# A two-block transformer forward pass: the feed-forward transposes go from TensorE to VectorE and device memory

## The chip, the cores and the metric

The kernel runs on one core of a Trainium2 chip. The metric is the device time of one execution in microseconds. A core has a matrix engine (TensorE, in the rows PE, with PEld for its weight loads), two engines for elementwise work that the kernel uses all the time (VectorE: DVE; ScalarE: ACT), a third one (GpSimd: POOL), an engine that here only issues transfers (SyncE: SP), and 16 DMA engines that move data between device memory and the on-chip memory (SBUF). TensorE writes into PSUM, eight banks of 128 x 512 floats.

## The reference

Two blocks run one after the other on 256 tokens of width 1024, all in float32. The first has a recurrent mixer and a differential attention, a feed-forward network with a squared ReLU (1024 to 4096 to 1024) and a gated embedding. The second has two layers, and each is a gated feed-forward network, an attention mixer and a second gated feed-forward network. The part that the change touches is this one, four times the gated form and once the squared ReLU:

```python
D_FF_2 = 2816
def swiglu(x, w_gate, w_up, w_down):
    return (jax.nn.silu(x @ w_gate) * (x @ w_up)) @ w_down

x = x + jnp.square(jax.nn.relu(h @ w_ff1[i])) @ w_ff2[i]            # first block, once
x = x + 0.5 * swiglu(rms_norm(x, norm_ffn1[layer]), w_gate, w_up, w_down)   # second block, four times
```

## The kernel before

**Products in three parts.** Each float32 product is made of three matrix products on a reduced type: an operand is split into `hi` (ScalarE copies it with rounding, L373) and `lo` (VectorE subtracts, L374), and TensorE adds hi x hi, lo x hi and hi x lo (`mm3`, all at L287).

**Weights.** They stream from device memory in units of 128 x 1024 floats (512 KB). SyncE issues the load into one of three `raw` buffers (L349), ScalarE and VectorE split it into `hi` and `lo`, and 11 pairs of those buffers stand ready for TensorE. A raw buffer comes free when `lo` is made, a pair when TensorE has used it for the last time.

**The feed-forward network (`mlp`).** The hidden width is cut into chunks: eight of 512 for the squared ReLU, and 512, 512, 512, 256, 512, 512 for each gated one. For each chunk TensorE makes a pass of 24 matrix products for each of the two token tiles t = 0, 1 and each of the input matrices (gate and up, or the one of the squared ReLU). ScalarE applies the activation to the first result (`a`, L471), and VectorE multiplies it with the second (`a`, L473). The chunk's `a` has to be turned around before it can stand as the stationary operand of the down product: `flip_side` queues four 128 x 128 transposes on TensorE (`tr`, L291), which a later `mm3` lets in between two of its products; then ScalarE and VectorE split the result from PSUM into `aTh` and `aTl`. The down product of a chunk comes one chunk later (`held`), after that chunk's own passes; the last two chunks are done together at the end.

**What sets the order.** TensorE runs in the order in which the program emits its work. A small model of time in the program (`Weave`, with a clock `t` that each matrix product moves on) decides where a queued side piece such as a transpose is let in. The other engines' queues are ordered by the framework's scheduler, when the program is built.

Of the kernel before, what the change touches and what calls it, by code (L numbers as in the profile page):

```python
# [7 lines left out]
F32 = mybir.dt.float32  # L8
# [4 lines left out]
AF = mybir.ActivationFunctionType  # L13
ALU = mybir.AluOpType
# [94 lines left out]
class Mark:  # L109


    def __init__(self):
        self.done, self.at, self.res = False, 0.0, None
# [105 lines left out]
class Ker:  # L219


    def __init__(self, ctx, tc, d):
        self.tc, self.nc, self.d = tc, tc.nc, d
        nc = self.nc
        ctx.enter_context(tc.manual_schedule(engines={mybir.EngineType.PE}))
        self.W = Weave()
        self.const = ctx.enter_context(tc.tile_pool(name="const", bufs=1))
        self.small = ctx.enter_context(tc.tile_pool(name="small", bufs=2))
        self.line_up(ctx, "a", 48)
        self.xp = ctx.enter_context(tc.tile_pool(name="xp", bufs=1))  # L230
        self.act = ctx.enter_context(tc.tile_pool(name="act", bufs=2))
        self.ps = ctx.enter_context(tc.tile_pool(name="ps", bufs=1, space=PSUM))
        self.banks = Slots(self.W, self.ps, "b", [128, 512], 8)
        self.quota, self.held = 2, 0
        self.x = [self.xp.tile([128, D], F32, name=f"x{t}") for t in range(2)]
        self.pre = None
# [135 lines left out]
    def split(self, hi, lo, src):  # L372
        self.nc.scalar.activation(out=hi, in_=src, func=AF.Copy)  # L373
        self.nc.vector.tensor_tensor(out=lo, in0=src, in1=hi.bitcast(F32), op=ALU.subtract)  # L374
# [63 lines left out]
    def flip_side(self, src, hi, lo, lat, wait=()):  # L438
# [8 lines left out]
        s.res = (hi, lo)  # L447
        return s

    def mlp(self, pool, hT, names, i, chunks, kind, res, after):

        nc, W = self.nc, self.W
        self.quota = 6
        acc = {}
        held = []
        nw = len(names) - 1
        for ci, w in enumerate(chunks):
            kt = w // 128  # L460
            ws = [self.wblock((n, i, ci)) for n in names[:-1]]
            order = [(t, j) for t in range(2) for j in range(nw)] if ci == 0 else [(t, j) for j in range(nw) for t in range(2)]
            a, aT = {}, {}
            for t, j in order:
                b = self.bank()
                p = b[1][:, :w]
                for k in range(8):
                    self.mm3(p, hT[t].at(k), ws[j][k], k == 0, k == 7)
                if j == 0:
                    a[t] = pool.tile([128, 512], F32, tag="a", name="a", bufs=4)[:, :w]  # L470
                    nc.scalar.activation(out=a[t], in_=p, func=AF.Silu if kind == "swiglu" else AF.Relu, scale=hT[t].r)  # L471
                if j == nw - 1:
                    nc.vector.scalar_tensor_tensor(out=a[t], in0=p, scalar=hT[t].r, in1=a[t], op0=ALU.mult, op1=ALU.mult)  # L473
                    th = pool.tile([128, 4, 128], F32R, tag="aTh", name="aTh", bufs=5)
                    tl = pool.tile([128, 4, 128], F32R, tag="aTl", name="aTl", bufs=5)
                    aT[t] = self.flip_side(a[t], th[:, :kt], tl[:, :kt], 3.0)
                self.drop(b, 2.0)
            held.append((kt, aT, self.wblock((names[-1], i, ci))))
            if 1 <= ci < len(chunks) - 1:
                for t in range(2):  # L480
                    self.down(acc, t, held[:1], res)
                held = held[1:]
        for t in range(2):
            self.down(acc, t, held, res, after)
# [1378 lines left out]
```

## Time and profile before

| | us |
|---|---|
| three timed runs, median (lowest, highest) | 1516.84 (1516.67, 1520.73) |
| the profiled execution | 1517.79 |
| its span, first to last instruction | 1516.0 |
| TensorE busy, matrix products | 1473.4 (97%) |
| VectorE busy | 927.7 (61%) |
| ScalarE busy | 760.7 (50%) |
| GpSimd busy | 46.9 (3%) |

An engine's busy share says how much of the span it worked. Matrix products overlap at their ends, so TensorE's time is better read from when one product starts to when the next one does. The five feed-forward networks take 940.6 us of the span.

### The profile page before, as it was taken

To read this page: it belongs to the slowest core of one execution; us is meant where nothing else is said; L and a number is where in the kernel's file an instruction comes from. 1 tells how busy PE (TensorE), PEld (TensorE's weight loads), DVE (VectorE), ACT (ScalarE), POOL (GpSimd) and SP (SyncE) were. 2 spreads that over 40 slices of the span, in tenths; PEclk is the share of its full clock that TensorE was granted. 3 is DMA by queue.
4 is the path that set the end of the run, shared out by engine and by line. 5 is a ranking of instruction groups with operands and counts; after the bars stand their busy time and mean duration, and the time that the engine had idled before them with its cause. 6 is when DMAs were issued, how large, how long until landed. Compare 5 with 4: busy or idle time off the path is not lost.

```text
span 1516.0 us, 22441 instructions
## 1 busy us (share of the span) xinstructions
PE 1473.4 (97%) x8804; PEld 1235.3 (81%) x8804; DVE 927.7 (61%) x1529; ACT 760.7 (50%) x1142; POOL 46.9 (3%) x70
## 2 busy tenths in 40 slices
PE   7899988999999999999999999999999999999999
PEld 6887767888888778887888888887888878888887
DVE  5885778755558755558546554565545787565552
ACT  6644445544446544436665444445444566464441
POOL 1120100000000000001100000000000010000000
PEclk9999999999999999999999999999999999999999
DMA  7233338655554765545434756547565444276551
GB/s 254 87 121 108 101 113 272 203 191 187 181 167 140 229 204 193 186 145 195 137 101 140 220 184 196 187 146 235 183 195 189 139 158 128 82 223 193 177 186 55
DMA packets 76298, 254.97 MB, mean 168 GB/s; under 512 B 11040, under 2 KB 13344, under 8 KB 76192
## 3 DMA queue, kind: packets, MB, share of 16 engines
q1 hardware_dynamic: 76192, 253.53, 51.8%
q8 instruction: 69, 1.13, 0.3%
q14 instruction: 37, 0.30, 0.1%
HBM read 252.45 MB, written 1.05 MB: 167 GB/s over the span
## 4 chain that ended last, share of the span: by engine, by line
PE 79%; DVE 7%; DMA 6%; ACT 5%; issue 2%; SPq 0%; POOL 0%; ACTq 0%; DVEq 0%; POOLq 0%
PE b L287 75%; DMA raw<-in_w_dram 5%; PE b L291 4%; DVE lo L374 3%; ACT hi L373 2%; DMA grow<-in_norm_mix_g_dram 0%; DMA stage<-in_consts_dram 0%; DMA lam<-in_lam_k_dram 0%; ACT L380 0%; DVE c L1141 0%; POOL rb L572 0%; DVE U L1269 0%; POOL rb L571 0%; DVE u L1138 0%; ACT e L384 0%
## 5 line engine op out<-in xcount | busy, mean ns | idle before, releaser
L374 DVE TENSOR_TENSOR lo<-raw,hi 128x1024 fp32r<-128x1024 f32 (+1 forms) x465 | 562.0, 1215 | 356.1 <-ACT hi L373 347.1
L373 ACT ACTIVATE hi<-raw 128x1024 fp32r<-128x1024 f32 (+1 forms) x465 | 486.0, 1050 | 415.8 <-PE b L287 207.1
L287 PE MATMUL b<-hi,hTh 128*128 128x512 f32 (+2 forms) x1312 | 495.6, 378 | 0.5 <-ACT hi L373 0.5
L287 PE MATMUL b<-lo,hTh 128*128 128x512 f32 (+2 forms) x1312 | 484.7, 369 | 0.8 <-DVE lo L374 0.8
L287 PE MATMUL b<-hi,hTl 128*128 128x512 f32 (+2 forms) x1312 | 484.9, 370 | 0.1
L287 PEld LDWEIGHTS b<-hi,hTl 128*128 128x128 f32 x1312 | 247.5, 189 | 43.1 <-DVE hTl L374 0.6
L287 PEld LDWEIGHTS b<-hi,hTh 128*128 128x128 f32 x1312 | 247.6, 189 | 42.0 <-issue 2.7
L287 PEld LDWEIGHTS b<-lo,hTh 128*128 128x128 f32 x1312 | 248.0, 189 | 40.0 <-DVE lo L374 1.7
L287 PE MATMUL b<-hi,aTh 128*128 128x512 f32 x480 | 191.4, 399 | 0.0
L287 PE MATMUL b<-lo,aTh 128*128 128x512 f32 x480 | 187.3, 390 | 0.0
L287 PE MATMUL b<-hi,aTl 128*128 128x512 f32 x480 | 187.2, 390 | 0.0
L287 PEld LDWEIGHTS b<-hi,aTl 128*128 128x128 f32 x480 | 90.2, 188 | 19.8
L287 PEld LDWEIGHTS b<-lo,aTh 128*128 128x128 f32 x480 | 90.3, 188 | 17.4
L287 PEld LDWEIGHTS b<-hi,aTh 128*128 128x128 f32 x480 | 90.2, 188 | 17.5
L471 ACT ACTIVATE a<-b,rsi_x 128x512 f32<-128x512 f32 (+1 forms) x52 | 34.4, 662 | 54.0 <-PE b L287 54.0
L373 ACT ACTIVATE aTh<-b 128x512 fp32r<-128x512 f32 (+1 forms) x64 | 36.3, 567 | 39.5 <-PE b L291 38.5
L473 DVE SCALAR_TENSOR_TENSOR a<-b,rsi_x,a 128x512 f32<-128x512 f32 (+1 forms) x52 | 37.3, 717 | 28.4 <-PE b L287 15.9
L287 PE MATMUL b<-hi,hT1h 128*128 128x512 f32 (+1 forms) x128 | 53.5, 418 | 0.0
L374 DVE TENSOR_TENSOR aTl<-b,aTh 128x512 fp32r<-128x512 f32 (+1 forms) x64 | 41.8, 653 | 17.2 <-ACT aTh L373 16.9
L287 PE MATMUL b<-lo,hT1h 128*128 128x512 f32 (+1 forms) x128 | 47.7, 372 | 0.6 <-DVE lo L374 0.6
L287 PE MATMUL b<-hi,hT1l 128*128 128x512 f32 (+1 forms) x128 | 47.4, 371 | 0.0
L374 DVE TENSOR_TENSOR hTl<-b,hTh 128x512 fp32r<-128x512 f32 (+1 forms) x48 | 29.2, 619 | 23.5 <-ACT hTh L373 23.5
(583 smaller groups left out, 1289.0 us busy)
## 6 DMA issues: line engine op xcount, KB each, us to landing
raw<-in_w_dram SPq DMA_DIRECT2D x446, 512.0 KB, 4.2
raw<-in_w_dram SPq DMA_DIRECT2D x16, 384.0 KB, 3.4
grow<-in_norm_ffn_dram SPq DMA_DIRECT2D x4, 512.0 KB, 5.0
x<-in_x_dram SPq DMA_DIRECT2D x4, 256.0 KB, 5.5
x<-in_x_dram SPq DMA_DIRECT2D x2, 512.0 KB, 4.3
grow<-in_norm_mix_dram SPq DMA_DIRECT2D x2, 512.0 KB, 4.5
out_dram<-x SPq DMA_DIRECT2D x4, 256.0 KB, 2.0
raw<-in_w_dram SPq DMA_DIRECT2D x2, 396.0 KB, 3.5
```

The costliest lines, as they stand in the source:

```text
L287: self.nc.tensor.matmul(out=out, lhsT=lhsT, rhs=rhs, start=start, stop=stop, skip_group_check=skip)
L291: self.nc.tensor.transpose(out=out, in_=src, identity=self.ident)
L373: self.nc.scalar.activation(out=hi, in_=src, func=AF.Copy)
L374: self.nc.vector.tensor_tensor(out=lo, in0=src, in1=hi.bitcast(F32), op=ALU.subtract)
L471: nc.scalar.activation(out=a[t], in_=p, func=AF.Silu if kind == "swiglu" else AF.Relu, scale=hT[t].r)
L473: nc.vector.scalar_tensor_tensor(out=a[t], in0=p, scalar=hT[t].r, in1=a[t], op0=ALU.mult, op1=ALU.mult)
```

## The change

The `a` of most chunks no longer passes TensorE. `flip_moved` lets VectorE transpose the 32 x 32 blocks of `a` into a buffer `fsq`, GpSimd's queue writes that to a scratch tensor `fmid` in device memory, and four more transfers of GpSimd's queue, one for each 32 partitions, read it back into `fto` with the blocks in their transposed places. ScalarE and VectorE then split `fto` (in SBUF) instead of a PSUM bank. Those splits are emitted later, in the next chunk: before its second pass, or before its fourth in chunk 1 of a gated network. The last chunk of each network, and chunk 0 of the squared ReLU, keep TensorE's transposes. So 52 of 64 turned tiles change path: 44 of width 512 (four transposes each) and 8 of width 256 (two each), 192 transposes in all.

```diff
+        self.dram = ctx.enter_context(tc.tile_pool(name="dram", bufs=3, space=bass.MemoryType.DRAM))
+    def flip_moved(self, pool, src, hi, lo):
+        nc = self.nc
+        n = src.shape[1] // 128
+        sq = pool.tile([128, 4, 4, 32], F32, name="fsq", tag="fsq", bufs=2)[:, :, :n]
+        to = pool.tile([128, 4, 4, 32], F32, name="fto", tag="fto", bufs=2)[:, :, :n]
+        nc.vector.transpose(out=sq.rearrange("p j k s -> p k j s"), in_=src.rearrange("p (k j s) -> p k j s", j=4, s=32))
+        mid = self.dram.tile([4, 32, 4, 128 * n // 4], F32, name="fmid", tag=f"fmid{n}")
+        nc.gpsimd.dma_start(out=mid.rearrange("i r j e -> (i r) j e"), in_=sq.rearrange("p j k s -> p j (k s)"))
+        for j in range(4):
+            nc.gpsimd.dma_start(out=to[32 * j:32 * j + 32].rearrange("r i k s -> r i (k s)"), in_=mid[:, :, j].rearrange("i r e -> r i e"))
+        v = lambda x: x.rearrange("p k (i s) -> p i k s", s=32)
+        m = Mark()
+        def split():
+            nc.scalar.activation(out=v(hi), in_=to, func=AF.Copy)
+            nc.vector.tensor_tensor(out=v(lo), in0=to, in1=v(hi).bitcast(F32), op=ALU.subtract)
+            m.res = (hi, lo)
+            self.W.finish(m, 4.0)
+        m.split = split
+        return m
...
-            for t, j in order:
+            landed, moved = moved, []
+            for n, (t, j) in enumerate(order):
+                if n == (1 if ci > 1 else 3):
+                    for m in landed:
+                        m.split()
...
-                    aT[t] = self.flip_side(a[t], th[:, :kt], tl[:, :kt], 3.0)
+                    if ci == len(chunks) - 1 or ci < 2 - nw:
+                        aT[t] = self.flip_side(a[t], th[:, :kt], tl[:, :kt], 3.0)
+                    else:
+                        aT[t] = self.flip_moved(pool, a[t], th[:, :kt], tl[:, :kt])
+                        moved.append(aT[t])
```

TensorE's order loses the 192 transposes and is otherwise the same, and so is SyncE's. Three queues change by more. ScalarE's queue, from chunk 4 to chunk 5 of the third network (`a` is an activation, the first one here that of chunk 4 and tile 1; `hi<-raw` a weight's split; `aTh` the split of a turned tile), before:

```order
508 L471 ACTIVATE a<-b,rsi_x 128x512
509 L373 ACTIVATE hi<-raw 128x1024 x3
510 L373 ACTIVATE aTh<-b 128x512
511 L373 ACTIVATE hi<-raw 128x1024 x2
512 L373 ACTIVATE aTh<-b 128x512
513 L373 ACTIVATE hi<-raw 128x1024 x2
514 L471 ACTIVATE a<-b,rsi_x 128x512
```

and with the change:

```order
508 L499 ACTIVATE a<-b,rsi_x 128x512
509 L374 ACTIVATE hi<-raw 128x1024 x5
510 L466 ACTIVATE aTh<-fto 128x4x4x32
511 L374 ACTIVATE hi<-raw 128x1024 x2
512 L466 ACTIVATE aTh<-fto 128x4x4x32
513 L499 ACTIVATE a<-b,rsi_x 128x512
514 L374 ACTIVATE hi<-raw 128x1024 x3
```

The two splits of a turned tile moved down by two weight splits, still ahead of the next chunk's first activation, and they now wait for a transfer instead of for TensorE.

VectorE's queue at the same place (`a` is the gating product, `fsq` the block transpose, `lo` and `aTl` the second halves of the splits), before:

```order
856 L473 SCALAR_TENSOR_TENSOR a<-b,rsi_x,a 128x512
857 L374 TENSOR_TENSOR lo<-raw,hi 128x1024 x2
858 L374 TENSOR_TENSOR aTl<-b,aTh 128x512
859 L473 SCALAR_TENSOR_TENSOR a<-b,rsi_x,a 128x512
860 L374 TENSOR_TENSOR lo<-raw,hi 128x1024 x2
861 L374 TENSOR_TENSOR aTl<-b,aTh 128x512
```

and with the change:

```order
894 L501 SCALAR_TENSOR_TENSOR a<-b,rsi_x,a 128x512
895 L457 STREAM_TRANSPOSE fsq<-a 128x4x4x32
896 L375 TENSOR_TENSOR lo<-raw,hi 128x1024 x2
897 L501 SCALAR_TENSOR_TENSOR a<-b,rsi_x,a 128x512
898 L457 STREAM_TRANSPOSE fsq<-a 128x4x4x32
899 L375 TENSOR_TENSOR lo<-raw,hi 128x1024 x2
900 L467 TENSOR_TENSOR aTl<-fto,aTh 128x4x4x32
901 L375 TENSOR_TENSOR lo<-raw,hi 128x1024 x2
902 L467 TENSOR_TENSOR aTl<-fto,aTh 128x4x4x32
```

A block transpose stands right behind each gating product, and `aTl` moved down.

GpSimd's queue, from the end of the recurrent mixer on, before (the `rb` rows belong to the first attention layer of the second block):

```order
41 L1399 TENSOR_TENSOR z<-x_77,bonus 128x256
42 L1400 TENSOR_TENSOR z<-z,row_g_1203 128x256
43 L571 TENSOR_TENSOR rb<-qn,gs 128x8x32
44 L572 TENSOR_TENSOR rb<-qn,gs 128x8x32
45 L571 TENSOR_TENSOR rb<-qn,gs 128x8x32
```

and with the change, where 110 transfers stand ahead of the first `rb`:

```order
41 L1431 TENSOR_TENSOR z<-x_79,bonus 128x256
42 L1432 TENSOR_TENSOR z<-z,row_g_1205 128x256
43 L459 DMA fmid<-fsq 128x512
44 L461 DMA fto<-fmid 32x4x128 x4
45 L459 DMA fmid<-fsq 128x512
46 L461 DMA fto<-fmid 32x4x128 x4
```

GpSimd had nothing to do in the feed-forward networks, and now issues five transfers there for each turned tile, 260 in all; the four reads wait for their write to have landed.

## Rows read from the trace of the kernel before

**Rows 1.** Windows over the five feed-forward networks: the sum over all of them.

```profile
sum 940.60, PE 934.48 PEld 778.38 DVE 530.11 ACT 439.81 POOL 0.00; mean PE 186.90 PEld 155.68 DVE 106.02 ACT 87.96 POOL 0.00
```

**Rows 2.** Chain that ended last, within the third feed-forward network: shares by line.

```profile
by line: PE b L287 96.3%; PE b L291 3.7%
```

**Rows 3.** Timeline of PE around four transposes: start, duration, instruction.

```profile
865.82 0.39 PE L287 MATMUL b<-hi,aTl 128*128 128x512 f32 x1
866.05 0.60 PE L291 MATMUL b<-ident,a 128*128 128x128 f32 x4
...
869.26 0.39 PE L287 MATMUL b<-hi,aTh 128*128 128x512 f32 x1
...
872.44 0.39 PE L287 MATMUL b<-hi,aTl 128*128 128x512 f32 x1
```

**Rows 4.** Timeline of PE around two transposes of a 256 chunk.

```profile
922.60 0.39 PE L287 MATMUL b<-hi,aTl 128*128 128x512 f32 x1
...
926.06 0.39 PE L287 MATMUL b<-lo,aTh 128*128 128x512 f32 x1
```

**Rows 5.** Timeline of PE, waits in the networks: in brackets the idle time.

```profile
511.72 0.66 PE L291 MATMUL b<-ident,a 128*128 128x128 f32 x4 [2.87 <-DVE a L473]
...
524.53 0.39 PE L287 MATMUL b<-lo,hTh 128*128 128x512 f32 x1
...
547.31 0.66 PE L291 MATMUL b<-ident,a 128*128 128x128 f32 x4 [1.24 <-DVE a L473]
...
1034.06 0.50 PE L287 MATMUL b<-lo,hTh 128*128 128x512 f32 x1 [0.76 <-DVE lo L374]
```

**Rows 6.** Timeline of DVE in the second network's chunk 1.

```profile
521.78 1.23 DVE L374 TENSOR_TENSOR lo<-raw,hi 128x1024 fp32r<-128x1024 f32 x1 [0.35 <-ACT hi L373]
```

**Rows 7.** Groups by line and shape: busy, mean ns, idle before.

```profile
L374 DVE TENSOR_TENSOR lo<-raw,hi 128x1024 fp32r<-128x1024 f32 x446 | 544.1, 1226 | 353.4 <-ACT hi L373 344.5
...
L373 ACT ACTIVATE hi<-raw 128x1024 fp32r<-128x1024 f32 x446 | 470.3, 1060 | 403.6 <-PE b L287 198.6 <-DMA raw<-in_w_dram 195.5 <-DVE lo L374 4.9
...
L373 ACT ACTIVATE aTh<-b 128x512 fp32r<-128x512 f32 x56 | 33.2, 594 | 32.7 <-PE b L291 31.7
...
L471 ACT ACTIVATE a<-b,rsi_x 128x512 f32<-128x512 f32 x46 | 31.6, 686 | 51.8 <-PE b L287 51.8
...
L918 DVE TENSOR_TENSOR h<-x,grow 128x512 f32<-128x512 f32 x32 | 22.1, 690 | 4.9 <-DMA grow<-in_norm_mix_g_dram 4.1
```

**Rows 8.** Timeline of DVE, third network: tile 0's gating product in chunks 1 and 4.

```profile
858.45 0.75 DVE L473 SCALAR_TENSOR_TENSOR a<-b,rsi_x,a 128x512 f32<-128x512 f32 x1
...
947.12 0.75 DVE L473 SCALAR_TENSOR_TENSOR a<-b,rsi_x,a 128x512 f32<-128x512 f32 x1 [1.32 <-PE b L287]
```

**Rows 9.** Timeline of PE, third passes of chunks 2 and 5: last unit's first use.

```profile
889.21 0.39 PE L287 MATMUL b<-lo,hTh 128*128 128x512 f32 x1
...
973.98 0.39 PE L287 MATMUL b<-lo,hTh 128*128 128x512 f32 x1
```

**Rows 10.** Timeline of POOL, DVE and SP in the first attention layer.

```profile
741.43 1.76 DVE L374 TENSOR_TENSOR lo<-raw,hi 128x1024 fp32r<-128x1024 f32 x1
742.08 1.71 POOL L572 TENSOR_TENSOR rb<-qn,gs 128x256 f32<-128x256 f32 x1
743.22 0.33 SPq L349 DMA_DIRECT2D raw<-in_w_dram  x1
...
751.02 0.73 POOL L572 TENSOR_TENSOR rb<-qn,gs 128x256 f32<-128x256 f32 x1
```

**Rows 11.** DMA: the queue's load and issues by size, with median us to landing.

```profile
q1 hardware_dynamic: 76192, 253.53, 51.8%
...
x<-in_x_dram SPq DMA_DIRECT2D x4, 256.0 KB, 5.5
...
out_dram<-x SPq DMA_DIRECT2D x4, 256.0 KB, 2.0
...
ident<-in_consts_dram SPq DMA_DIRECT2D x1, 64.0 KB, 3.2
```

More of the change, by code (lines that the diff above doesn't have):

```diff
@@ L456, in mlp @@
         acc = {}
-        held = []
+        held, moved = [], []
         nw = len(names) - 1
```

## The prediction, as put on record

> **What bounds the kernel now.** I read the windows over the five feed-forward networks first, since the change touches nothing else: TensorE is busy for 934.5 of 940.6 us there, VectorE for 530.1, ScalarE for 439.8 [rows 1]. A busy PE need not be PE at its best, so the chain of waits comes next: inside the third network the chain is TensorE alone, 96.3% products and 3.7% at L291, the transposes [rows 2]. A microsecond taken off TensorE's queue there is a microsecond of the kernel, as long as weights and turned tiles keep arriving in time. Third, PE's timeline around a group of transposes gives their price, and fourth, the waits say where something else was late.
>
> **What is removed.** In steady flow one product starts every (872.44 - 869.26)/14 = 0.227 us [rows 3]. From the last product before four transposes (865.82) to the thirteenth behind them (869.26) it takes 3.44 us, where 13 steps take 2.95 [rows 3]. So a group of four costs 0.49 us, less than the 0.60 us that the group shows as duration, because its ends overlap. Around two transposes, 14 steps take 926.06 - 922.60 = 3.46 us instead of 3.18: 0.28 us [rows 4]. The sum is 44 x 0.49 + 8 x 0.28 = 23.8 us.
>
> Three waits change it. In the second network TensorE stands 2.87 us before a moved group, since VectorE is late with `a` [rows 5]. Without the group it goes on, but into weights that are hardly ahead: the `lo` that it uses at 524.53 is ready at 521.78 + 1.23 = 523.01, 1.52 us early [rows 5, 6]. Coming 2.87 + 2 x 0.49 = 3.85 us sooner it would wait 2.33 there, so 0.5 of the 2.87 is kept. The 1.24 us wait before another moved group I count whole. In the fourth network, chunk 1, TensorE already waits for a `lo` [rows 5]; the 2 x 0.49 us saved just before it only lengthen that wait: -1.0. Together 23.8 + 0.5 + 1.2 - 1.0 = 24.5 us.
>
> **What is added, and what hides it.** VectorE gets 52 block transposes, which the trace does not show. The nearest row is a pass of VectorE over 128 x 512 from SBUF to SBUF, 0.69 us [rows 7]; twice that is my upper bound, and nothing excludes it. At 0.69, and about 0.4 for the narrow ones, this is 33.6 us: VectorE goes from 530 to 564 of 941 us, 60%, and its idle time hides it. The splits read SBUF instead of PSUM; I count no difference. The transfers move 2 x 0.26 MB for each wide tile. The load queue takes 0.518 x 1516 / 253.5 = 3.1 us of all 16 engines per MB [rows 11], so 1.6 us a tile and, for 48 wide tiles' worth, 78 us: eight points on a queue at 52%. That lies beside loads that wait for free buffers; with no cover it would cost 1.6 us a tile.
>
> **The added wait, which decides.** ScalarE now stands at `aTh` until the round trip has landed, and behind it wait two weight splits, the next tile's split, the next activation and three more weight splits. TensorE waits for those in turn. I take the tightest place, chunk 4 to 5 of the third network. The first product `a` starts at 947.12 and takes 0.75 [rows 8]; with the block transpose the trip starts at 948.6. TensorE wants the unit that is split first behind the next activation at 973.98 [rows 9]. Behind the second tile's landing ScalarE needs 0.59 for `aTh`, 0.69 for the activation, 1.06 for that unit's `hi`, and VectorE 1.23 for `lo` [rows 7], 3.6 us; TensorE comes 1.0 us sooner for the two groups. The second tile has to land by 969.4, 20.8 us behind the first one's start. Between two wide chunks, 1 to 2, the trip starts at 858.45 + 0.75 + 0.69 = 859.9 [rows 8], two more `hi` stand behind the second tile's split (2.1 us, so 5.7 in all), and the unit is wanted at 889.21 [rows 9]: 22.6 us. I take that for 22 of the 26 chunks with moved tiles, the squared ReLU's six among them, and 20.8 for four.
>
> How long is it? GpSimd's queue is in order: an issue, the wait for the write, four issues, then the second tile's five. With i for an issue, w for the write and r for the last read, the second tile lands at 2(w + 5i) + r. Neither issue from GpSimd nor such a read is in the trace. For i the bounds are SyncE's issue, 0.33, and GpSimd's longest pass over 128 x 256, 1.71 [rows 10]; I take GpSimd's short pass, 0.73, as an issue reads no tile. For w the bounds are 2.0, the output's write of the same size, and 5.5, a load of it; I take 2.0, the same direction. For r a 64 KB load took 3.2 [rows 11], and I take that; 2.0 and 5.5 bound it too. That gives 2(2.0 + 3.65) + 3.2 = 14.5 us, with 6 to spare. All lower bounds give 2(2.0 + 1.65) + 2.0 = 9.3, all upper ones 2(5.5 + 8.55) + 5.5 = 33.6, 11 to 13 too late at each of the 26 chunks, some 290 us. So I count the wait at nothing, and its cover is the weights that stand ready.
>
> The Trainium skill, DMA: Bandwidth & Descriptors, Anatomy of one DMA, fits a GpSimd-issued transfer by 2.0 us and bytes over 436 GB/s. By that, an estimate, the write takes 2.6 and a read 2.2 us, end to end; with 0.73 for i the sum would be 14.7. No run here shows it.
>
> **Time.** The profiled execution took 1517.79 us, span 1516.0; 1517.8 - 24.5 = 1493.3. The median of the three runs is 0.95 us lower than the profiled one, so the forecast is 1492. What a measurement of this kernel can tell from no change is about 0.3%, 4.6 us.
>
> **Rivals.** (1) *Part is given back at the networks' starts.* GpSimd and VectorE hold each other up: beside GpSimd's pass a `lo` took 1.76 us instead of 1.23 [rows 7, 10]. If each issue delays a `lo` by the 0.53, two tiles' ten issues and two transposes cost VectorE 6.7 us a chunk. Elsewhere 44% of VectorE's time is idle [rows 1], but in chunk 1 weights were as little as 0 to 1.5 us ahead [rows 5, 6]; five such places give up to 34 us. At half of it the time is 1509. For it: the rows named. Against: an issue may touch no tile. Chance 0.13.
>
> (2) *Slower: the round trip is late at every chunk.* The place is `aTh` in ScalarE's queue. GpSimd's pass took 1.71 us beside VectorE's `lo` and 0.73 with VectorE free [rows 10]. If each issue waits so, i = 1.71, the trip takes 2(2.0 + 8.55) + 3.2 = 24.3 us, 1.7 late at 22 chunks and 3.5 late at 4: 51 us, giving 1492 + 51 = 1543. It decides against the change from i = 1.6 on: at 23.3 us the trip costs 22 x 0.7 + 4 x 2.5 = 25 us, what the transposes gave. The Trainium skill, SBUF — State Buffer, the box on the trap "DVE blocks DMA", has a rule that speaks for this: VectorE in a mode that holds the shared ports keeps GpSimd from writing descriptors, and the transfer seems to wait for VectorE. By it the time would be near the 1543; rows 10 show such a wait for GpSimd's passes, and none for a transfer. The page limits the case of two SBUF inputs, `lo`'s, to GpSimd work that reads SBUF. Chance 0.15.
>
> (3) *No change: TensorE's freed time turns into waiting for weights.* Then the network would be paced by loads, and the time stay at 1512 to 1521. Against: ScalarE's `hi` waits as much for TensorE to free a pair (198.6 us) as for loads (195.5) [rows 7], and a load queue at 52% can carry the 2.6% faster pace [rows 11]. Chance 0.07.
>
> **How the numbers follow.** The forecast has 0.65 and its own range is 1487 (rows 5's wait of 2.87 kept whole, and no loss in chunk 1: 24.5 + 2.4 + 1.0 = 28, and the spread of the runs) to 1499 (a fifth of rival 1's 34 us). The range for 8 in 10 takes in rivals 1 and 3, leaves out the 0.15 of rival 2: 1487 to 1520. Faster: 0.65 and most of rival 1, 0.75. Same: rival 3 and the rest of rival 1 that ends there, 0.09. Slower: rival 2 and rival 1's end, 0.16.
>
> **What would show it.** Right: PE busy falls by about 24 us at unchanged products; the windows of the five networks are each 4 to 6 us shorter; no wait of PE in their steady part; GpSimd's issues last under 1.2 us; the second tile lands within 15 us. ScalarE may show waits of some us for `fto`, which cost nothing as long as TensorE shows none. Wrong: PE waits for `hi` or `lo` right behind a split of `fto` at each chunk (rival 2), PE waits in chunk 1 alone and `lo` longer than 1.3 us (rival 1), or PE's idle time grown by what its transposes lost, with ScalarE waiting for loads (rival 3). The prediction fails if an issue or the write takes over twice what I took.

## The result, and the profile after

| | before | after |
|---|---|---|
| median of 4 runs each, us (lowest, highest) | 1516.76 (1515.12, 1520.73) | 1538.53 (1534.02, 1543.68) |
| the profiled execution, us | 1517.79 | 1543.68 |
| its span, us | 1516.0 | 1541.9 |

The ratio is 1.0143, with a 95% interval of 1.0127 to 1.0159. The kernel is slower by some 22 us, where 24.5 us of gain were forecast. The profiled execution is the slowest of its four, 5.2 us above the median, so what the profile shows as lost is some 5 us more than what the medians show. Of the executions below, one at 2072.78 us (moved chunks 2 to 4) and one of the kernel before at 2270.23, with a granted TensorE clock of 0.655 and 0.602, are left out of every median and ratio.

The changed kernel's line numbers differ from those of before: products are L288, TensorE's transposes L292, weight splits L374 and L375, `a` L499 and L501, and in `flip_moved` the block transpose is L457, the write L459, the reads L461, the splits L466 and L467. The busy times on its page (us, share of the span, instructions):

```profile
PE 1469.9 (95%) x8612; PEld 1224.5 (79%) x8612; DVE 956.1 (62%) x1581; ACT 749.8 (49%) x1142; POOL 191.0 (12%) x330
```

TensorE lost its 192 transposes, but only 3.5 us of busy time. The windows over the same five networks, their sum, which answers to [rows 1]:

```profile
sum 967.30, PE 931.41 PEld 767.96 DVE 558.01 ACT 427.24 POOL 144.36; mean PE 186.28 PEld 153.59 DVE 111.60 ACT 85.45 POOL 28.87
```

The networks take 26.7 us longer than the 940.60 of before, and the span 25.9. TensorE was idle for 6.1 us in them and now is for 35.9. The chain of waits inside the third network, by line, which answers to [rows 2]:

```profile
by line: DMA raw<-in_w_dram 28.5%; PE b L288 14.3%; issue 14.3%; ACT hi L374 10.2%; DVE lo L375 9.7%; DMA fto<-fmid 7.7%; DMA fmid<-fsq 7.5%; POOL fto L461 4.7%; PE b L292 1.2%; DVE a L501 1.1%; DVE fsq L457 0.7%; ACT a L499 0.6%; ACT junk 
```

It was TensorE alone. Now weight loads, weight splits and the round trip stand in it, and TensorE has 15.5%. The waits of the kernel after (us in total, times, longest):

```profile
ACT hi L374 <- DMA raw<-in_w_dram: 301.8, 194, 6.2
...
ACT aTh L466 <- DMA fto<-fmid: 178.6, 48, 7.3
DVE aTl L467 <- ACT aTh L466: 140.8, 47, 6.5
...
ACT hi L374 <- PE b L288: 53.7, 50, 3.1
...
PE b L288 <- ACT hi L374: 16.4, 6, 5.1
...
PE b L288 <- DVE lo L375: 11.6, 18, 1.1
```

ScalarE stands at the splits of turned tiles for 178.6 us in 26 chunks, 6.9 us a chunk. The groups by line and shape, which answer to [rows 7]:

```profile
L375 DVE TENSOR_TENSOR lo<-raw,hi 128x1024 fp32r<-128x1024 f32 x446 | 539.2, 1223 | 252.1 <-ACT hi L374 248.8
L374 ACT ACTIVATE hi<-raw 128x1024 fp32r<-128x1024 f32 x446 | 464.2, 1057 | 353.5 <-DMA raw<-in_w_dram 296.8 <-PE b L288 45.3 <-DVE lo L375 7.1
...
L457 DVE STREAM_TRANSPOSE fsq<-a 128x512 f32<-128x512 f32 x44 | 31.3, 710 | 1.2
...
L466 ACT ACTIVATE aTh<-fto 128x512 fp32r<-128x512 f32 x44 | 27.8, 632 | 153.1 <-DMA fto<-fmid 153.1
```

ScalarE's `hi` waits for loads for 296.8 us instead of 195.5, and for TensorE to free a pair for 45.3 instead of 198.6. The weights no longer stand ready.

**Where the time went.** I cut each network at the start of one pass in its last chunk: the second input matrix and tile 0, or tile 1 in the squared ReLU. The windows from there to the network's end, summed over all five, in the kernel before:

```profile
sum 167.14, PE 167.14 PEld 138.19 DVE 87.86 ACT 58.51 POOL 0.00; mean PE 33.43 PEld 27.64 DVE 17.57 ACT 11.70 POOL 0.00
```

and after, with the third and fourth network (length, busy times, PEclk, DMA share, GB/s):

```profile
971.33:1015.35 44.02, 38.23 (x164) 30.13 (x163) 26.23 (x37) 19.38 (x27) 2.18 (x4) 0.92 0.45 150
1168.85:1215.89 47.04, 40.27 (x164) 31.68 (x163) 23.83 (x36) 17.39 (x26) 1.15 (x3) 0.89 0.40 130
...
sum 210.67, PE 182.81 PEld 145.34 DVE 109.87 ACT 78.45 POOL 6.13; mean PE 36.56 PEld 29.07 DVE 21.97 ACT 15.69 POOL 1.23
```

The last stretches grew by 43.5 us. All that lies ahead of them shrank from 773.5 to 756.6 us, by 16.8, where the transposes gave 24.5. So of 51 us lost, 43.5 lie in these last stretches. TensorE stands idle for 27.9 of the 43.5 (210.67 - 182.81); the other 15.7 are busy time (182.81 instead of 167.14) for the same products, at a granted clock of 0.89 to 0.96 in the five stretches instead of 1.00. The last section shows such a place.

**That place in the third network.** ScalarE's timeline from chunk 3's splits to chunk 5's:

```profile
939.68 0.42 ACT L466 ACTIVATE aTh<-fto 128x256 fp32r<-128x256 f32 x1 [5.32 <-DMA fto<-fmid]
...
946.30 0.42 ACT L466 ACTIVATE aTh<-fto 128x256 fp32r<-128x256 f32 x1 [3.35 <-DMA fto<-fmid]
...
954.76 1.06 ACT L374 ACTIVATE hi<-raw 128x1024 fp32r<-128x1024 f32 x1 [0.50 <-DMA raw<-in_w_dram]
...
970.63 0.63 ACT L466 ACTIVATE aTh<-fto 128x512 fp32r<-128x512 f32 x1 [5.42 <-DMA fto<-fmid]
...
977.95 0.63 ACT L466 ACTIVATE aTh<-fto 128x512 fp32r<-128x512 f32 x1 [4.78 <-DMA fto<-fmid]
...
979.05 2.99 ACT L374 ACTIVATE hi<-raw 128x1024 fp32r<-128x1024 f32 x3
```

VectorE's (its gating product of chunk 4, tile 0, is the `a`):

```profile
955.86 1.22 DVE L375 TENSOR_TENSOR lo<-raw,hi 128x1024 fp32r<-128x1024 f32 x1 [0.92 <-ACT hi L374]
957.00 0.74 DVE L501 SCALAR_TENSOR_TENSOR a<-b,rsi_x,a 128x512 f32<-128x512 f32 x1
957.78 0.71 DVE L457 STREAM_TRANSPOSE fsq<-a 128x512 f32<-128x512 f32 x1
```

GpSimd's, which issues the trip:

```profile
958.78 0.56 POOL L459 DMA_DIRECT2D fmid<-fsq  x1 [15.83 <-DVE fsq L457]
964.06 2.18 POOL L461 DMA_DIRECT2D fto<-fmid  x4 [4.71 <-DMA fmid<-fsq]
966.23 0.56 POOL L459 DMA_DIRECT2D fmid<-fsq  x1
972.28 2.18 POOL L461 DMA_DIRECT2D fto<-fmid  x4 [5.49 <-ACT hi L374]
```

and TensorE's:

```profile
949.34 0.39 PE L288 MATMUL b<-hi,hTl 128*128 128x512 f32 x1
...
973.53 0.50 PE L288 MATMUL b<-lo,hTh 128*128 128x512 f32 x1 [0.46 <-DVE lo L375]
...
980.15 0.79 PE L288 MATMUL b<-hi,hTh 128*128 128x512 f32 x1 [3.81 <-ACT hi L374]
981.41 0.79 PE L288 MATMUL b<-lo,hTh 128*128 128x512 f32 x1 [0.47 <-DVE lo L375]
982.00 0.63 PE L288 MATMUL b<-hi,hTl 128*128 128x512 f32 x1
...
985.41 0.53 PE L288 MATMUL b<-lo,hTh 128*128 128x512 f32 x1
```

Read them from TensorE's side. It starts the last product of tile 0's second pass in chunk 4 at 949.34, but VectorE's gating product starts only at 957.00. It stands in order behind a `lo` that waited for a `hi` that waited for a load, and the load was late because ScalarE had stood 5.32 and 3.35 us at chunk 3's splits, and while it stands the three raw buffers fill up and no further load is issued. So the trip starts some 7 us late. The second tile is there at 977.95, and its splits have held back the three `hi` behind 979.05, the first of which TensorE waits for at 980.15.

### The profile page after: what moved, and what is told of

The parts are those of the page before. It is cut to its first block, busy times and chain, and to the rows that moved or that the text cites. A ratio compares the mean times of both kernels' runs of the same rounds, so it can differ in the third digit from the quotient of the medians.

```text
span 1541.9 us, 22751 instructions
## 1 busy us (share of the span) xinstructions
PE 1469.9 (95%) x8612; PEld 1224.5 (79%) x8612; DVE 956.1 (62%) x1581; ACT 749.8 (49%) x1142; POOL 191.0 (12%) x330
## 4 chain that ended last, share of the span: by engine, by line
PE 35%; DMA 24%; issue 17%; DVE 12%; ACT 8%; POOL 4%; SPq 0%; ACTq 0%; POOLq 0%; DVEq 0%
PE b L288 33%; DMA raw<-in_w_dram 14%; DVE lo L375 6%; ACT hi L374 6%; DMA fto<-fmid 5%; DMA fmid<-fsq 4%; POOL fto L461 3%; PE b L292 2%; DVE a L501 1%; DMA grow<-in_norm_mix_g_dram 0%; ACT aTh L466 0%; POOL rb L603 0%; POOL rb L604 0%; ACT a L499 0%; DMA stage<-in_consts_dram 0%
## 5 line engine op out<-in xcount | busy, mean ns | idle before, releaser
L375 DVE TENSOR_TENSOR lo<-raw,hi 128x1024 fp32r<-128x1024 f32 (+1 forms) x465 | 556.9, 1211 | 254.7 <-ACT hi L374 251.3
L374 ACT ACTIVATE hi<-raw 128x1024 fp32r<-128x1024 f32 (+1 forms) x465 | 479.8, 1048 | 366.9 <-DMA raw<-in_w_dram 301.8
L288 PE MATMUL b<-hi,hTh 128*128 128x512 f32 (+2 forms) x1312 | 498.0, 380 | 16.4 <-ACT hi L374 16.4
L288 PE MATMUL b<-lo,hTh 128*128 128x512 f32 (+2 forms) x1312 | 490.8, 374 | 10.2 <-DVE lo L375 10.0
L288 PE MATMUL b<-hi,hTl 128*128 128x512 f32 (+2 forms) x1312 | 488.3, 372 | 0.6 <-DVE hTl L375 0.6
L288 PEld LDWEIGHTS b<-hi,hTh 128*128 128x128 f32 x1312 | 250.0, 191 | 62.0 <-ACT hi L374 19.8
L288 PEld LDWEIGHTS b<-lo,hTh 128*128 128x128 f32 x1312 | 250.5, 191 | 57.3 <-DVE lo L375 18.0
L288 PEld LDWEIGHTS b<-hi,hTl 128*128 128x128 f32 x1312 | 250.3, 191 | 43.4 <-DVE hTl L375 1.0
L288 PE MATMUL b<-hi,aTh 128*128 128x512 f32 x480 | 189.5, 395 | 0.8 <-ACT aTh L374 0.8
L288 PE MATMUL b<-hi,aTl 128*128 128x512 f32 x480 | 187.3, 390 | 0.6 <-DVE aTl L375 0.6
L288 PE MATMUL b<-lo,aTh 128*128 128x512 f32 x480 | 187.5, 391 | 0.0
L461 POOL DMA_DIRECT2D fto<-fmid x208 | 113.6, 553 | 205.0 <-DMA fmid<-fsq 95.7
L459 POOL DMA_DIRECT2D fmid<-fsq x52 | 30.9, 594 | 756.8 <-DVE fsq L457 329.9
L467 DVE TENSOR_TENSOR aTl<-fto,aTh 128x512 fp32r<-128x512 f32 (+1 forms) x52 | 33.9, 651 | 140.8 <-ACT aTh L466 140.8
L466 ACT ACTIVATE aTh<-fto 128x512 fp32r<-128x512 f32 (+1 forms) x52 | 31.2, 599 | 178.8 <-DMA fto<-fmid 178.6
L288 PEld LDWEIGHTS b<-hi,aTl 128*128 128x128 f32 x480 | 90.5, 189 | 20.4 <-DVE aTl L375 1.1
L288 PEld LDWEIGHTS b<-hi,aTh 128*128 128x128 f32 x480 | 90.6, 189 | 19.5 <-ACT aTh L374 1.2
L288 PEld LDWEIGHTS b<-lo,aTh 128*128 128x128 f32 x480 | 90.6, 189 | 18.2
L288 PE MATMUL b<-hi,hT1h 128*128 128x512 f32 (+1 forms) x128 | 53.5, 418 | 0.0
L288 PE MATMUL b<-lo,hT1h 128*128 128x512 f32 (+1 forms) x128 | 47.9, 374 | 0.6 <-DVE lo L375 0.6
L288 PE MATMUL b<-hi,hT1l 128*128 128x512 f32 (+1 forms) x128 | 47.5, 371 | 0.0
L375 DVE TENSOR_TENSOR hTl<-b,hTh 128x512 fp32r<-128x512 f32 (+1 forms) x48 | 29.2, 619 | 23.3 <-ACT hTh L374 23.3
```

What stands on the lines that cost most here:

```text
L288: self.nc.tensor.matmul(out=out, lhsT=lhsT, rhs=rhs, start=start, stop=stop, skip_group_check=skip)
L459: nc.gpsimd.dma_start(out=mid.rearrange("i r j e -> (i r) j e"), in_=sq.rearrange("p j k s -> p j (k s)"))
L461: nc.gpsimd.dma_start(out=to[32 * j:32 * j + 32].rearrange("r i k s -> r i (k s)"), in_=mid[:, :, j].rearrange("i r e -> r i e"))
L466: nc.scalar.activation(out=v(hi), in_=to, func=AF.Copy)
L467: nc.vector.tensor_tensor(out=v(lo), in0=to, in1=v(hi).bitcast(F32), op=ALU.subtract)
```

## Experiments

Two theories stood at first. *Queue*: ScalarE and VectorE stand at the splits of turned tiles, weight splits come late behind them, and the cover (the weights that stand ready, split) is not made good. *Contention*: the transfers slow the weight loads, or GpSimd and VectorE hold each other up.

**late.** The splits move behind the activation of the second gate pass (in the squared ReLU, of the first pass). They are pinned there in ScalarE's queue, because the framework's scheduler orders it.

```diff
-                if n == (1 if ci > 1 else 3):
-                    for m in landed:
-                        m.split()
+                if n == nw and landed:
+                    with self.tc.issue_after(act):
+                        for m in landed:
+                            m.split()
...
-                    nc.scalar.activation(out=a[t], in_=p, func=..., scale=hT[t].r)
+                    act = nc.scalar.activation(out=a[t], in_=p, func=..., scale=hT[t].r).ins
```

> Edit: the splits of the moved tiles stand later in ScalarE's queue, behind the activation of the chunk's second gate pass (squared ReLU: of its first pass); all transfers stay. Queue theory (the loss is that ScalarE and VectorE stand at the split of a turned tile, 178.6 us in all, and the weight splits behind it come late; three raw buffers refill the cover only slowly): ScalarE's wait at that split falls from 178.6 to under 20 us, the last chunk's second up pass loses its 6 to 8 us per network, the time goes to 1493 to 1502 us. Contention theory (the transfers slow the weight loads, or GpSimd and VectorE hold each other up): nothing of that changes, 1525 to 1540.

Measured: 1496.6 us, ratio 0.9868 (0.9840 to 0.9896). ScalarE's wait at the split in this kernel:

```profile
ACT aTh L466 <- DMA fto<-fmid: 3.0, 3, 1.2
```

The windows over its last stretches, the sum:

```profile
sum 167.13, PE 167.13 PEld 138.21 DVE 93.93 ACT 64.22 POOL 0.00; mean PE 33.43 PEld 27.64 DVE 18.79 ACT 12.84 POOL 0.00
```

All 43.5 us are back, with every transfer in place. The queue theory holds for them.

**no_transfer.** The block transposes without the trip.

```diff
-        to = pool.tile([128, 4, 4, 32], F32, name="fto", tag="fto", bufs=2)[:, :, :n]
...
-        mid = self.dram.tile([4, 32, 4, 128 * n // 4], F32, name="fmid", tag=f"fmid{n}")
-        nc.gpsimd.dma_start(...)
-        for j in range(4):
-            nc.gpsimd.dma_start(...)
+        to = sq
```

> Edit: no transfers; the split reads what VectorE's block transposes left, so the blocks are not moved between partitions (that part of the computation is left out). Queue and contention theory both expect TensorE's freed time in full, 1490 to 1497. A third theory (the block transposes, or splits that read SBUF, cost what was lost) expects 1510 or more.

Measured: 1491.18 us, ratio 0.9832 (0.9804 to 0.9859). The windows over its five networks:

```profile
sum 914.80, PE 911.51 PEld 759.90 DVE 559.48 ACT 438.08 POOL 0.00; mean PE 182.30 PEld 151.98 DVE 111.90 ACT 87.62 POOL 0.00
```

That is 25.8 us less than before. The third theory falls: VectorE's added work (957.1 us busy in this kernel, 927.7 before) costs nothing that shows.

**transfers_idle.** TensorE keeps its transposes, the trip is made, and nobody waits.

```diff
-                        aT[t] = self.flip_moved(pool, a[t], th[:, :kt], tl[:, :kt])
-                        moved.append(aT[t])
+                        self.flip_moved(pool, a[t], th[:, :kt], tl[:, :kt])
+                        aT[t] = self.flip_side(a[t], th[:, :kt], tl[:, :kt], 3.0)
```

> Edit: TensorE keeps all its transposes as before, and the block transposes and all five transfers of each of the 52 tiles are made as well, but nobody reads what they bring. Queue theory: nothing waits for them, so within 5 us of the kernel before, 1517 to 1522. Contention theory: the loss of the change without its gain, 1535 to 1562.

Measured: 1524.8 us, ratio 1.0046 (1.0023 to 1.0069). It lies between the two expectations, far nearer to the first. The five networks take 947.8 us, 7.2 more than before. One place of it, in the second network's chunk 0, where [rows 5] has 2.87:

```profile
512.91 0.66 PE L292 MATMUL b<-ident,a 128*128 128x128 f32 x4 [3.85 <-DVE a L501]
```

Contention is real, then, but costs about 7 us; the distance from late to no_transfer, 5.4 us, agrees. It does not show in the weight loads' median, which is 4.2 us from issue to landing in the kernel before, in the changed one and here; the longest load took 6.8, 7.7 and 8.0 us. Nor does a weight's `lo` take longer here, 1224 ns against 1226.

**raw5.** Five raw buffers and ten pairs.

```diff
+        self.rawx = ctx.enter_context(self.tc.tile_pool(name="rawx", bufs=2))
...
+        rawp = self.rawx if len(self.hls) > 1 and self.turn % 5 in (1, 3) else self.rawp
-        raw = self.rawp.tile([128, self.unit], F32, tag="raw", name="raw")
+        raw = rawp.tile([128, self.unit], F32, tag="raw", name="raw")
...
-    K.more_weights(ctx, 6)
+    K.more_weights(ctx, 5)
```

> Edit: from the first network on five raw buffers and ten pairs of hi and lo instead of three and eleven; the splits wait as they did. Queue theory: loads go on for two more units while ScalarE stands, and the cover is refilled faster (a unit per about 1.4 us instead of 2.3), so most of the loss comes back: 1496 to 1512. Contention theory: no gain or a further loss, since more loads run beside the transfers: 1530 to 1545.

Measured: 1505.49 us, ratio 0.9930 (0.9904 to 0.9956). Its waits:

```profile
ACT aTh L468 <- DMA fto<-fmid: 284.9, 52, 10.8
...
ACT hi L376 <- PE b L288: 141.6, 144, 5.2
...
ACT hi L376 <- DMA raw<-in_w_dram: 33.7, 29, 5.5
```

ScalarE stands longer at the split than in the changed kernel, 284.9 us against 178.6, and yet the kernel is 33 us faster. The wait itself is not the price. The price is weights that are not ready afterwards. Here `hi` waits 33.7 us for loads, where the changed kernel has 301.8, and 141.6 us for TensorE to free a pair instead of 53.7: the weights stand ready again.

**before_raw5.** The same edit of the buffers, made to the kernel before.

> Edit to the kernel before: five raw buffers and ten pairs from the first network on, no moved transposes. A control for the run with five raw buffers. Queue theory: the kernel before has no long wait to bridge, so it stays within 4 us, 1513 to 1521. If five raw buffers are worth some 30 us by themselves (loads were short of buffers anyway): 1485 to 1500.

Measured: 1510.15 us, ratio 0.9948 (0.9924 to 0.9972). Below what the theory allowed: five buffers are worth 7.6 us without any moved tile. If the two add up, the other 25 of raw5's 33 us belong to the round trips.

**late_raw5.** Both edits.

> Edit: late splits and five raw buffers with ten pairs together. Queue theory: the late splits already took the wait away; what is left of the distance to the run without transfers (5 us) is weights barely ahead in the first chunks while transfers run, where two more buffers help a little: 1490 to 1497. If five buffers help independently of the wait: 1480 to 1489. If ten pairs are too few with late splits: above 1500.

Measured: 1489.84 us, ratio 0.9812 (0.9790 to 0.9834), the fastest kernel of all. That is just under the first range and above the second. From late to here the ratio falls by 0.0056, about the 0.0052 that five buffers give the kernel before; so they seem to help by themselves, and not only where the first chunks are short of weights.

**How many waits it takes.** The second tile of chunk 4 was there 19.5 us behind the first one's block transpose (977.95 - 958.49), and the prediction allowed 20.8. So I asked whether the trip at this place is too long by itself, or only after other waits. The edit, here for chunk 4 alone:

```diff
-                    if ci == len(chunks) - 1 or ci < 2 - nw:
+                    if nw == 1 or ci != 4:
```

> Edit: only chunk 4 of each gated network is moved, 8 tiles in all; the others and the squared ReLU keep TensorE's transposes. Two forms of the queue theory. Compound: one trip fits (the second tile lands 18 to 19.5 us behind the first one's block transpose, 20.8 are allowed), the loss came because earlier waits had used up the cover and made VectorE's gating product, and with it the trip, 4 to 9 us late; here each network keeps its 0.98 us and the time is 1510 to 1516. Single: the trip at this place is too long by itself, each network loses 6 to 8 us in the last chunk's second up pass, 1536 to 1546.

> Edit: only chunks 3 (256 wide) and 4 of each gated network are moved, 16 tiles. Compound: ScalarE's wait behind chunk 3 makes the trip of chunk 4 start late, and part of the loss appears, 2 to 6 us a network against 1.5 gained: 1518 to 1535, and slower than the kernel with chunk 4 alone. Single: the loss of chunk 4 alone less 0.56 a network, so 2 us faster than that kernel.

> Edit: chunks 2, 3 and 4 of each gated network are moved, 24 tiles; the others and the squared ReLU keep TensorE's transposes. Without any loss the transposes give 4 x 2.5 us: 1507. Compound (each wait takes more from the cover than the loads give back before the next): a part of the loss, 1508 to 1520, with VectorE's gating product of chunk 4 some us late. From the start (the cover is lost at chunks 0 and 1, where weights are barely ahead, and never comes back): no loss here, 1505 to 1509.

> Edit: as before, with chunks 1 to 4 of each gated network, 32 tiles. Without any loss 1503. Compound: most of the loss of the whole change, 4 to 8 us a network: 1518 to 1535. From the start: chunk 0's part is missing, so little is lost: 1502 to 1512.

> Edit: chunks 0 to 3 of each gated network, 32 tiles; chunk 4 and the last one keep TensorE's transposes. Without any loss 1503. Both: the large loss in the last chunk's second up pass (6 to 8 us a network) needs the trip of chunk 4, so it is gone; what is lost in chunks 1 to 3 shows: 1503 to 1512.

Measured, in us. "Lost" is how far the gain falls short of what the moved transposes cost before (0.49 or 0.28 us each group): once from the networks' sum in the profile, once from the medians. The wait and the last stretches are from the profiled executions, which lie up to 5.6 us from their medians (chunks 1 to 4: 1526.01).

| moved in the gated networks | median | ratio (95%) | ScalarE's wait at the split | last stretches | lost, profile | lost, medians |
|---|---|---|---|---|---|---|
| 4 | 1512.91 | 0.9970 (0.9954 to 0.9987) | 29.4 | 167.17 | 0.2 | -0.9 |
| 3 and 4 | 1511.47 | 0.9958 (0.9943 to 0.9974) | 54.4 | 168.82 | 3.5 | -0.1 |
| 2 to 4 | 1515.85 | 0.9998 (0.9973 to 1.0023) | 98.7 | 178.33 | 12.2 | 9.2 |
| 1 to 4 | 1520.40 | 1.0020 (1.0000 to 1.0039) | 134.4 | 188.20 | 23.2 | 17.7 |
| 0 to 4, and the squared ReLU (the change) | 1538.53 | 1.0143 (1.0127 to 1.0159) | 178.6 | 210.67 | 50.5 | 45.6 |
| 0 to 3 | 1529.13 | 1.0073 (1.0052 to 1.0093) | 94.9 | 167.16 | 22.9 | 26.4 |

Chunk 4 alone loses nothing: "single" falls. ScalarE still stands there, in the third network for 3.38 and 4.07 us:

```profile
956.38 0.63 ACT L466 ACTIVATE aTh<-fto 128x512 fp32r<-128x512 f32 x1 [3.38 <-DMA fto<-fmid]
...
963.04 0.63 ACT L466 ACTIVATE aTh<-fto 128x512 fp32r<-128x512 f32 x1 [4.07 <-DMA fto<-fmid]
```

and VectorE's gating product there waits for TensorE, and for nothing else:

```profile
945.12 0.75 DVE L501 SCALAR_TENSOR_TENSOR a<-b,rsi_x,a 128x512 f32<-128x512 f32 x1 [1.41 <-PE b L288]
945.90 0.71 DVE L457 STREAM_TRANSPOSE fsq<-a 128x512 f32<-128x512 f32 x1
```

"Compound" is right in direction, but I had it too quick: one wait ahead costs next to nothing (3 and 4 was not slower than 4 alone, as it expected), chunks 2 and 1 then add some 9 us each, and the last step 28 by the medians, with chunk 0 and the squared ReLU in it. ScalarE's and VectorE's queues from chunk 4 to 5 are in the same order in the five kernels that move chunk 4, so what differs there is the waits ahead. "From the start" falls too, since chunks 1 to 4 lose 18 to 23 us without chunk 0.

Chunks 0 to 3 missed what both expected, 1503 to 1512. The last stretch is whole, as expected, but 22.9 us are lost ahead of it. Chunk 4's transposes are on TensorE again, and there they wait for the late gating product:

```profile
631.74 0.63 PE L292 MATMUL b<-ident,a 128*128 128x128 f32 x4 [4.02 <-DVE a L501]
...
640.56 0.63 PE L292 MATMUL b<-ident,a 128*128 128x128 f32 x4 [1.13 <-DVE a L501]
```

VectorE's rows ahead of the first of these waits:

```profile
629.71 1.23 DVE L375 TENSOR_TENSOR lo<-raw,hi 128x1024 fp32r<-128x1024 f32 x1 [0.65 <-ACT hi L374]
630.85 0.75 DVE L501 SCALAR_TENSOR_TENSOR a<-b,rsi_g,a 128x512 f32<-128x512 f32 x1
```

This shows the second way in which the delay reaches TensorE: VectorE is late with `a`, because it works through late `lo` first. ScalarE stands no longer here than with chunks 2 to 4 (94.9 us against 98.7), and more is lost; so the standing alone does not give the loss, and where it falls counts as well. How much of it is chunk 0's own, I did not separate, so this loss is placed but not fully explained.

## Why the prediction was wrong

**What was right.** The transposes were worth what the rows said: 24.5 us forecast, 25.8 in no_transfer, where TensorE's busy time also falls by the 24.0 us from 1473.4 to 1449.4. The block transpose was sized rightly, and VectorE's added time is hidden. In the groups above it took 710 ns against the 0.69 us forecast, the split from SBUF 632 ns against 594 from PSUM, and `lo` 1223 ns, as before.

**Terms that were off in size.** The changed kernel's issues (KB each, median us to landing):

```profile
fmid<-fsq POOLq DMA_DIRECT2D x44, 256.0 KB, 4.6
fto<-fmid POOLq DMA_DIRECT2D x176, 64.0 KB, 4.1
```

and GpSimd's time for each issue of a read and of a write (ns, lowest, median, highest):

```profile
L461 POOL DMA_DIRECT2D fto<-fmid x208: 551/551/584, 307.5 to 1497.3; - x104
L459 POOL DMA_DIRECT2D fmid<-fsq x52: 563/563/755, 302.4 to 1490.1; - x52
```

So i was 0.55 us instead of 0.73, w 4.6 instead of 2.0 and r 4.1 instead of 3.2: the trip 2(4.6 + 5 x 0.55) + 4.1 = 18.8 us instead of 14.5. The row that I took for w, the output's write, stands at the kernel's end, behind the last weight load; the nearest row by what goes on beside it would have been a load in the stream, and the upper bound of 5.5 was nearer. The prediction gave a write of over twice its 2.0 us as a sign that it fails, and 4.6 is that. But 18.8 is still inside the 20.8 allowed, and chunk 4 alone confirms that one such trip fits. The transfers' cost beside other work was counted at nothing and is about 7 us.

The Trainium skill, DMA: Bandwidth & Descriptors, Anatomy of one DMA, gave estimates of 2.6 us for the write and 2.2 for a read; the medians of 4.6 and 4.1, beside a stream of weights, decide against them here.

**The step that failed** is "So I count the wait at nothing, and its cover is the weights that stand ready". Two things in it were wrong. It set each trip against the lead that the weights have in the kernel before, place by place, as if every chunk found the cover whole. And it let the trip start right behind TensorE's pass, though VectorE's gating product stands in the same queue as the weight splits and is late when they are. SyncE's queue in the changed kernel shows how slowly the cover comes back; eight weight loads in a row behind a wait, first issue to the end of the last:

```profile
951.48 15.35 SPq L350 DMA_DIRECT2D raw<-in_w_dram  x8
```

That is (15.35 - 0.33) / 7 = 2.15 us a unit, and three buffers give that: a load lands 4.2 us after its issue (median), `hi` takes 1.06 and `lo` 1.22, and a third of the 6.5 is 2.2, an estimate. TensorE needs one per 12 products, 2.72 us, so 0.57 us a unit is won back, and at most 6.8 us in the 12 units of a wide chunk. That is an estimate of the best case, without any further standing. ScalarE stood 6.9 us a chunk on average, and while it stands the three raw buffers fill up and loading stops (SyncE issues a load at 966.50, and the next at 973.51). So nothing is over for the cover; and when it is gone the trips start late, and TensorE waits. Two more raw buffers, or splits that nobody has to stand for, end most of it: raw5 and late.

The mis-sized trip may have a part in this, which no run separates. At the 14.5 us forecast, ScalarE would stand some 4.3 us less a chunk, 2.6 us by the same estimate, and that the loads could win back. No run has a shorter trip with the splits in their place, so how much of the loss would be left then stays open.

**The rivals.** The time came near rival 2's 1543, but by another way. Its place is right, `aTh` in ScalarE's queue. Its mechanism, issues held up to 1.71 us by VectorE, is not there: the longest issue of a read took 584 ns and of a write 755. The rule of the Trainium skill that I set beside it (SBUF — State Buffer, the box on the trap "DVE blocks DMA") does not show in these issues either, with VectorE busy for 62% of the span. Whether it has a part in the longer landings, no run separates. Rival 1 put a loss at the networks' starts, and the place shown from transfers_idle is one; that run loses a fifth of the rival's 34 us. Its mechanism, a longer `lo`, is not there, as the 1224 ns show. Rival 3's sign was there, ScalarE waiting for loads, and my argument against it was the wrong one: the load queue's 52% do not decide it, since the loads are limited by three buffers and the time that each is held (five buffers bring the wait for loads from 301.8 to 33.7 us).

## What to carry to other kernels

A wait that fits the lead of a prefetch once may not fit it every time: set the standing time per round against what the prefetch wins back per round (buffers over their holding time, not the queue's bandwidth). Before a wait on a transfer goes into an in-order queue, look at everything that the same queue feeds, the start of that transfer too; queue it behind an instruction that is later anyway.

## What the runs showed of the hardware

The granted clock of TensorE fell during one wait of 3.81 us. Windows of the changed kernel around it (PEclk is the third number from the right):

```profile
976.00:980.00 4.00, 0.34 (x2) 0.00 (x0) 0.69 (x1) 2.05 (x3) 0.00 (x0) 0.86 0.57 183
980.00:984.00 4.00, 3.38 (x7) 2.39 (x8) 3.50 (x3) 2.62 (x4) 0.00 (x0) 0.50 0.39 132
...
988.00:992.00 4.00, 4.00 (x22) 3.27 (x21) 1.65 (x2) 1.61 (x4) 0.00 (x0) 1.00 0.76 253
```

At 0.50, the lower level of 1.2 GHz, eight products from 982.00 to 985.41 start every 0.43 us instead of 0.227. In this last stretch 9.2 us were lost, of which TensorE's waits are 0.46 + 3.81 + 0.47 and a later one of 1.06, 5.8 in all; the products at the lower clock hold most of the rest. So these waits cost TensorE more than their own length. In the last stretches of all five networks, 15.7 us of added busy time stand beside 27.9 us of added idle time.
